# Weighted sum of two expert outputs: a ScalarE product in the first tile, and the last tile's stores as four pieces from SyncE's queue

## The chip, the cores and the metric

The kernel runs on one core of a Trainium2 chip. The core has five engines, of which this kernel computes with two: VectorE (DVE in the profile) and ScalarE (ACT). SyncE (SP) and ScalarE also issue transfers between the device memory (HBM) and the on-chip memory (SBUF); what each has issued stands in a queue of its own (in the profile q1 holds what SP issued, q10 what ScalarE issued), and 16 DMA engines work on both queues. The metric is the device time of one execution in microseconds (us); the time of a kernel is the median over its runs.

## The reference

For each of 16 x 1024 tokens there are two rows of 512 float32 numbers (the outputs of two experts) and two weights. The result is the weighted sum of the two rows.

```python
# expert_outputs (16, 1024, 2, 512), combine_weights (16, 1024, 2), all float32
weights = combine_weights[..., np.newaxis]
return np.sum(expert_outputs * weights, axis=2).astype(np.float32)
```

So 67.1 MB are read, 33.6 MB are written, and there are three floating-point operations for each number written.

## The kernel before, in words

The 16384 tokens are laid over 128 partitions: partition p holds tokens 128p to 128p + 127. All weights are loaded once into `wt` (line 43, issued from ScalarE's queue, 128 KB).

The loop of line 45 goes over 16 tiles of J = 8 tokens per partition. A tile is loaded by one transfer of 4 MB into `et` (line 48, issued from SP). Each of its 8 tokens then takes two instructions on 128x512 elements:

- the product of the first expert's row and its weight, written to `ot`: on VectorE in tiles 0 to 14 (line 57), on ScalarE in the last tile (line 55);
- the product of the second row and its weight, added to it, in one VectorE instruction (line 58).

Tiles 0 to 14 leave by one store of 2 MB each (line 66, issued from ScalarE's queue). The last tile leaves in three stores of 4, 2 and 2 tokens (1 MB, 512 KB, 512 KB), from ScalarE's queue too. In the text, "load 15" is the load of the last tile, "store 14" the last 2 MB store, and tiles and loads count from 0.

Both pools hold four buffers (lines 39 and 40). So load g waits until VectorE is through with tile g - 4, and the products of tile g may only overwrite an `ot` that store g - 4 has read out. The framework puts the waits in and settles the order on each engine, which need not be that of the program text: in the last tile the trace shows six ScalarE products (tokens 0 to 5), then the stores of 4 and of 2 tokens, then the products of tokens 6 and 7, then the last store. An engine works through its own instructions in that order, so that a store that waits for VectorE holds the products behind it on ScalarE.

ScalarE needs a table in place before its first activation. The load of that table is an instruction that the compiler adds ahead of the first `activation` (it stands under line 55 too).

Of the kernel before, what the change touches and what calls it, by code (L numbers as in the profile page):

```python
# [1 line left out]

# [4 lines left out]


@with_exitstack
def kernel(  # L10
    ctx: ExitStack,
    tc: tile.TileContext,
    expert_outputs: bass.AP,
    combine_weights: bass.AP,
    out: bass.AP,
):


    nc = tc.nc
    b, s, k, h = expert_outputs.shape  # L20
    assert k == 2
    n = b * s
    P = nc.NUM_PARTITIONS
    per = n // P
    assert per * P == n
    eo = expert_outputs.rearrange("b s k h -> (b s) (k h)").rearrange("(p t) f -> p t f", p=P)
    cw = combine_weights.rearrange("b s k -> (b s) k").rearrange("(p t) k -> p (t k)", p=P)
    o = out.rearrange("b s h -> (b s) h").rearrange("(p t) f -> p t f", p=P)

    dt = mybir.dt.float32  # L30
    mult = mybir.AluOpType.mult
    add = mybir.AluOpType.add

    J = 8
    copy = mybir.ActivationFunctionType.Copy
    last = per // J - 1

    wpool = ctx.enter_context(tc.tile_pool(name="w", bufs=1))
    ipool = ctx.enter_context(tc.tile_pool(name="in", bufs=4))
    opool = ctx.enter_context(tc.tile_pool(name="out", bufs=4))  # L40

    wt = wpool.tile([P, per * k], dt)
    nc.scalar.dma_start(out=wt, in_=cw)

    for g in range(per // J):
        et = ipool.tile([P, J, k * h], dt)
        ot = opool.tile([P, J, h], dt)
        nc.sync.dma_start(out=et, in_=eo[:, g * J : (g + 1) * J, :])  # L48
        c0 = 0
        for c in (4, 2, 2) if g == last else (J,):  # L50
            for i in range(c0, c0 + c):
                t = g * J + i
                w0, w1 = wt[:, 2 * t : 2 * t + 1], wt[:, 2 * t + 1 : 2 * t + 2]
                if g == last:
                    nc.scalar.activation(out=ot[:, i, :], in_=et[:, i, 0:h], func=copy, scale=w0)  # L55
                else:
                    nc.vector.tensor_scalar_mul(out=ot[:, i, :], in0=et[:, i, 0:h], scalar1=w0)  # L57
                nc.vector.scalar_tensor_tensor(  # L58
                    out=ot[:, i, :],
                    in0=et[:, i, h : 2 * h],  # L60
                    scalar=w1,
                    in1=ot[:, i, :],
                    op0=mult,
                    op1=add,
                )
            nc.scalar.dma_start(  # L66
                out=o[:, g * J + c0 : g * J + c0 + c, :], in_=ot[:, c0 : c0 + c, :]
            )
            c0 += c


# [1 line left out]
_INS = ['expert_outputs', 'combine_weights']  # L73
_OUTS = [((16, 1024, 512), 'float32')]


# [23 lines left out]
```

## Time and profile before

Three runs took 241.24, 241.34 and 241.75 us; the median is 241.34 us. The profiled execution took 241.88 us, with a span of 240.1 us on the core, so 1.8 us lie around the span.

| What | us or rate |
|---|---|
| span of the profiled execution | 240.1 |
| VectorE busy | 133.8 (56%) |
| ScalarE busy | 6.4 (3%) |
| mean transfer rate over the span | 420 GB/s |
| weights in SBUF, VectorE's first instruction | 13.92 |
| first store issued | 22.51 |
| load 15 landed | 227.7 |
| table load, last tile | 227.81 to 229.09 |
| last store issued | 236.54 |

How to read it: times count from the start of the span. A row of groups names the line, the engine, the operation, what it writes and reads, the count, the busy time, the mean of one in ns, and the idle time of the engine ahead of it with what ended it. "Waits" are put down to what came last. The share of the DMA engines is the mean over the 16 of the time that their packets took; it can stand a little over 1, since packets overlap. A transfer's "time to landing" runs from its issue until the last of its 16 parts has reported. The row "queue 14, instruction" counts packets that carry instructions to the engines.

### The profile page before, as it was taken

The numbers are of one execution on the slowest core, as the hardware profiler recorded it, in microseconds if no ns is written. First come the engines' busy times: TensorE is split into PE (matmuls) and PEld (weight loads), VectorE is DVE, ScalarE is ACT, GpSimd is POOL, SyncE is SP. The second block draws the span as 40 slices with busy tenths as digits, with TensorE's granted clock in tenths as the row PEclk, the third lists the DMA queues.
The fourth block names the chain that finished last, engine by engine and source line by source line (L and its number), as shares of the span: only waits on it lengthen the run. The fifth ranks groups of instructions, "written<-read, shape, count | busy, mean of one in ns | idle before, by whom it ended". The sixth has DMA issues, their size and how long they took to land.

```text
span 240.1 us, 377 instructions
## 1 busy us (share of the span) xinstructions
DVE 133.8 (56%) x248; ACT 6.4 (3%) x9; POOL 0.2 (0%) x4
## 2 busy tenths in 40 slices
DVE  0068937729185490945819276391853919549062
ACT  0000000000000000000000000000000000000072
POOL 0000000000000000000000000000000000000000
DMA  7999999999999999999999999999999999999967
GB/s 267 439 434 431 355 434 456 414 431 437 437 423 445 439 409 426 456 415 453 420 437 431 415 448 423 431 450 437 435 423 434 420 429 442 418 450 437 412 296 304
DMA packets 5042, 100.81 MB, mean 420 GB/s; under 512 B 560, under 2 KB 688, under 8 KB 944
## 3 DMA queue, kind: packets, MB, share of 16 engines
q1 hardware_dynamic: 2304, 67.11, 65.4%
q10 hardware_dynamic: 2736, 33.69, 32.9%
q14 instruction: 2, 0.02, 0.0%
HBM read 67.24 MB, written 33.55 MB: 420 GB/s over the span
## 4 chain that ended last, share of the span: by engine, by line
DMA 56%; DVE 26%; another core or an unknown queue 13%; issue 1%; ACT 1%; SPq 0%; ACTq 0%; DVEq 0%
DMA et<-in_expert_outputs_dram 56%; DVE ot L58 16%; DVE ot L57 10%; ACT ot L55 1%; ACT L55 1%; SPq L48 0%; ACTq L66 0%; DVEq L95 0%; DVEq L57 0%; ACTq L55 0%
## 5 line engine op out<-in xcount | busy, mean ns | idle before, releaser
L57 DVE TENSOR_SCALAR ot<-et,wt 128x512 f32<-128x512 f32 x120 | 52.7, 482 | 93.4 <-DMA et<-in_expert_outputs_dram 79.5
L58 DVE SCALAR_TENSOR_TENSOR ot<-et,wt,ot 128x512 f32<-128x512 f32 x128 | 90.0, 746 | 9.3 <-ACT ot L55 9.3
L55 ACT ACT_TABLE_LOAD x1 | 1.3, 1283 | 227.8 <-DMA et<-in_expert_outputs_dram 227.8
L55 ACT ACTIVATE ot<-et,wt 128x512 f32<-128x512 f32 x8 | 5.1, 709 | 1.5 <-DVE ot L58 1.5
L84 POOL MEMSET const-bfloat16-1.0<- 128x1 bf16 x1 | 0.1, 101 | 0.0
L84 POOL MEMSET const-uint8-127<- 128x1 uint8 x1 | 0.1, 101 | 0.0
L84 POOL MEMSET const-float32-0.0<- 128x1 f32 x1 | 0.1, 98 | 0.2 <-issue 0.2
L84 POOL MEMSET const-float32-1.0<- 128x1 f32 x1 | 0.1, 98 | 0.0
## 6 DMA issues: line engine op xcount, KB each, us to landing
et<-in_expert_outputs_dram SPq DMA_DIRECT2D x16, 4096.0 KB, 49.6
out_dram<-ot ACTq DMA_DIRECT2D x15, 2048.0 KB, 24.9
out_dram<-ot ACTq DMA_DIRECT2D x1, 1024.0 KB, 3.9
out_dram<-ot ACTq DMA_DIRECT2D x2, 512.0 KB, 3.2
wt<-in_combine_weights_dram ACTq DMA_DIRECT2D x1, 128.0 KB, 13.2
```

The source lines that it names most:

```text
L55: nc.scalar.activation(out=ot[:, i, :], in_=et[:, i, 0:h], func=copy, scale=w0)
L57: nc.vector.tensor_scalar_mul(out=ot[:, i, :], in0=et[:, i, 0:h], scalar1=w0)
L58: nc.vector.scalar_tensor_tensor(out=ot[:, i, :], in0=et[:, i, h : 2 * h], scalar=w1, in1=ot[:, i, :], op0=mult, op1=add,)
L84: nc = _bacc.Bacc("TRN2", target_bir_lowering=False, num_devices=1)
```

## The change

Two things change. First, the product of token 0 of tile 0 goes from VectorE to ScalarE, by the same `activation` that the last tile uses; the compiler's table load then stands ahead of this one. Second, the last tile's stores are of 2, 2, 2 and 2 tokens (512 KB each) instead of 4, 2 and 2, and they are issued from SP's queue instead of ScalarE's. The sums, the other 119 VectorE products, the loads and the stores of tiles 0 to 14 stay as they were.

```diff
-        for c in (4, 2, 2) if g == last else (J,):
+        for c in (2, 2, 2, 2) if g == last else (J,):
             for i in range(c0, c0 + c):
                 t = g * J + i
                 w0, w1 = wt[:, 2 * t : 2 * t + 1], wt[:, 2 * t + 1 : 2 * t + 2]
-                if g == last:
+                if t == 0 or g == last:
                     nc.scalar.activation(out=ot[:, i, :], in_=et[:, i, 0:h], func=copy, scale=w0)
                 else:
                     nc.vector.tensor_scalar_mul(out=ot[:, i, :], in0=et[:, i, 0:h], scalar1=w0)
...
-            nc.scalar.dma_start(
+            (nc.sync if g == last else nc.scalar).dma_start(
                 out=o[:, g * J + c0 : g * J + c0 + c, :], in_=ot[:, c0 : c0 + c, :]
             )
```

More of the change, by code (lines that the diff above doesn't have):

```diff
@@ L32 @@
     add = mybir.AluOpType.add
+    copy = mybir.ActivationFunctionType.Copy
     J = 8
-    copy = mybir.ActivationFunctionType.Copy
     last = per // J - 1
```

## The prediction, made before the changed kernel ran

> **What bounds the kernel now.** I read the page first: the busy times, the slices of the span and the queues.
>
> ```profile
> DVE 133.8 (56%) x248; ACT 6.4 (3%) x9; POOL 0.2 (0%) x4
> ...
> DMA  7999999999999999999999999999999999999967
> GB/s 267 439 434 431 355 434 456 414 431 437 437 423 445 439 409 426 456 415 453 420 437 431 415 448 423 431 450 437 435 423 434 420 429 442 418 450 437 412 296 304
> ...
> q1 hardware_dynamic: 2304, 67.11, 65.4%
> q10 hardware_dynamic: 2736, 33.69, 32.9%
> q14 instruction: 2, 0.02, 0.0%
> ```
>
> VectorE idles 44% of the span; the DMA engines are busy in every slice but the first and the last two (0.98 of 16 engines' span). So the kernel moves bytes, and time can be won only where DMA engines stand idle: at the start, and in the last 12 us, where the rate falls to 296 and 304 GB/s. The change works on the last. The end of the chain of waits (start, length, what) shows how that stretch runs:
>
> ```profile
> 227.72 0.02 issue
> 227.74 0.04 ACTq L55
> 227.78 0.03 issue
> 227.81 1.28 ACT L55
> 229.09 0.01 issue
> 229.10 0.73 ACT ot L55
> 229.83 0.02 issue
> 229.85 4.08 DVE ot L58 x6
> 233.93 0.02 issue
> 233.95 0.34 ACTq L66
> 234.29 0.05 issue
> 234.34 0.73 ACT ot L55
> 235.07 0.03 issue
> 235.09 0.75 DVE ot L58
> ```
>
> Load 15 lands at 227.72. The table load (1.28 us) comes before the first product, and later ScalarE's products of tokens 6 and 7 stand behind the second store's issue, so that VectorE waits 1.17 us after its sixth sum. Read alone, this chain says that both waits can be taken out whole. I therefore asked what the DMA engines do meanwhile; the view by stretches of time gives the busy time of the engines, the clock, the DMA share and GB/s:
>
> ```profile
> 228.00:231.00 3.00, 1.15 (x2) 2.99 (x5) 0.00 (x0) 1.00 0.98 421
> 231.00:232.00 1.00, 1.00 (x3) 1.00 (x3) 0.00 (x0) 1.00 0.54 229
> 232.00:233.00 1.00, 1.00 (x2) 0.88 (x2) 0.00 (x0) 1.00 0.08 33
> 233.00:234.00 1.00, 0.92 (x2) 0.00 (x0) 0.00 (x0) 1.00 0.63 262
> 234.00:236.00 2.00, 0.91 (x2) 1.33 (x2) 0.00 (x0) 1.00 0.97 395
> ```
>
> After the load is in, older stores still fill the engines until 231 or so; a hole of about 1.5 us follows, and then the last tile's stores run at full rate to the end. But 0.08 in 232 to 233 is not zero: it is one of 16 engines, still at work. The trace's packet records, which no view prints, say so: 15 engines finish their part of store 14 between 231.4 and 232.6, the sixteenth at 233.36. The first packets of the last tile's stores start at 233.47 to 233.62 on all 16. For that engine there is hardly a hole, and a store has landed only when its slowest sixteenth has.
>
> Where its lag comes from: the two instruction packets (8 KB each) start at 47.4 and 173.7. Up to the load that landed at 168.7 the last of the 16 parts reports within 0.06 us of the one before it; from the load landed at 184.1 on it is 0.90 us behind. A fetch thus delays one engine by 0.85 to 0.9 us. The change takes away one of VectorE's instructions of 248, so I expect both fetches to stay.
>
> **The change part by part.** *The table load leaves the last tile:* ScalarE's first product there starts at 227.82 instead of 229.10, 1.28 us sooner.
>
> One rule can be weighed here. The Trainium skill, "ScalarE: Activation LUTs", section "What ACT_TABLE_LOAD costs", gives 1283 ns for the load, as this trace has it, and adds a drain of about 1380 ns, 2.66 us in total. By the page the first product would come 2.66 us sooner; the trace has the product 0.01 us after the load, with no drain between, so 1.28 is used. With 2.66 the limit by computing would move 1.38 us further, and the sum, which the slowest DMA engine sets, would stay.
>
> *The stores leave ScalarE's queue:* its eight products run through, and VectorE's 1.17 us wait goes. Six sums took 4.08 us, a step of (4.08 - 0.75)/5 = 0.666; eight take 5.41. First product 227.82 to 228.55, first sum at 228.57, eighth done at 233.98 instead of 236.51. Pieces are ready after sums 2, 4, 6 and 8: 229.98, 231.31, 232.65, 233.98.
>
> *Four issues on SP, three fewer on ScalarE:* SP's 328 ns row for a load's issue is near ScalarE's 338 for a store's. SP's last load issue ends at 177.7, and nothing but the final waits stands behind, so these issues hold nobody. The weights' issue and stores 0 to 14 stay in ScalarE's queue; POOL's four constants are over at 0.4. From issue to first packet took 0.84 us (232.63 to 233.47) and 0.87 (236.54 to 237.41). The old stores lie in q10, the new in q1; both take turns on the same 16 engines, so crossing over doesn't change what an engine has left to do.
>
> *The 1 MB store becomes two of 512 KB:* per engine 8 packets of 0.313 (2.50 us) become 16 of 0.160 (2.56): 0.06 us more, and one completion more (0.01). That this store's fixed time to landing adds to the end is bounded by zero (the pieces queue behind each other, as the second 512 KB did, landing 3.9 us after issue but 1.3 after the 1 MB) and by 2.6 - 1.3 = 1.3 us, the last store's 2.6 less its data time. I take zero, by the nearest row: the last tile's own queue.
>
> A rule speaks against this part. The Trainium skill, "DMA: Bandwidth & Descriptors", section "Rules for kernel authors", wants at least 1 MiB per DMA for full bandwidth, and its fit has 2.0 us fixed for each; paid once more and not overlapped, the time would come out near 243.0. The trace's two 512 KB stores ran at 385 to 395 GB/s behind a 1 MB one, so the sum has none of it.
>
> *Both limits of the tail.* By computing: last issue 234.01, first packet 234.88, eight packets 1.28: data out at 236.16 instead of 238.84, 2.68 us sooner. By the slowest engine: store 14 done at 233.36, then 4 x 8 packets of 0.160 and completions: 233.36 + 5.12 + 0.04 = 238.52, 0.32 us sooner. The later one decides: 0.3 us. Its other ends are 2.7 (no lagging engine) and 0, if some 0.3 us of gaps between pieces return.
>
> *The first tile's new wait.* The weights are there at 13.92; then ScalarE takes 1.28 and 0.73, so the first sum starts at 15.95. VectorE saves one product (0.44 in its pairs of 0.88) of the 8.56 us that tile 0 took (13.92 to 22.48). If it waits idle, it ends at 15.95 + 8.12 = 24.07, 1.6 late; if one product is put ahead of the wait, 1.15 late. Behind it stand load 4's issue (SP) and store 0's (ScalarE), both 1.15 to 1.6 us later than 22.51. Cover: loads 1 to 3 fill the queue until 52; tile 1 starts up to 0.6 later than 23.46, and VectorE then waits for load 2 until 37.74, so the delay is gone by tile 2. Work left undone by stores is done by loads, so cost zero. Without that cover it is up to 1.6 us; and a gain isn't excluded either: where the first store comes in, the rate falls to 311 and 336 GB/s (24 to 28 us), (430 - 324)/430 x 4 = 1.0 us lost against the usual 430. This may be lost again, in part, or doubled: -1.0 to +1.0. I take zero, since the same first store enters the same full queue.
>
> Sum: -0.3 on the profiled execution (span 240.1 to 239.8, time 241.88 to 241.6). That execution stands 0.54 above the median of 241.34, so the forecast for the median is 241.0.
>
> **The rivals.** *B, the lag is smaller.* If the engine that fetches isn't the one that is last anyway, the next slowest (232.58) decides: 0.78 us more, 240.3. For it: two fetches that land at another moment. Against: both fetches exist in any version.
>
> *C, computing decides.* If all engines are through by 232, the whole 2.7 us come: 238.7. Against it stands the record at 233.36.
>
> *D, slower: the first store's entry.* At 24 to 28 us, the later store 0 meets another phase of the loads; the dip grows, or the fetching engine falls in with those 0.8 us behind at landing (two or three engines are, from 37 on). A dip twice as long costs 1.0, net +0.7: 242.0. It decides from a loss of 0.8 us upward. For it: such a dip stands in the trace only there, and its cause isn't shown. Against: the engines have the same bytes.
>
> *E, nothing happens:* gaps eat the 0.3 us, 241.3.
>
> **How the numbers follow.** A measurement of this kernel can hardly tell less than 0.2% (0.48 us) from no change. Forecast A 0.45 (its own range 240.8 to 241.4, all within 0.2% but 0.03), B 0.24, C 0.08, D 0.17, E 0.06. Faster: B, C and 0.03 of A, 0.35. Same: 0.42 + 0.06 = 0.48. Slower: D, 0.17. For 8 in 10 the range leaves out C and most of D above 241.9, and takes in B with a 0.1 us margin: 240.2 to 241.9.
>
> **What would show it.** Table load at 14 us and none after 220; first sum near 15.9; load 4 and store 0 issued at 23.6 to 24.1; eight sums in 5.4 us without a gap; four issues on SP at 230.0 to 234.0; no slice under 0.3 DMA share before 237 but then a thinning tail, with one engine finishing alone near 238.5. Wrong, if the last pieces land with all engines together 1 us or more sooner (B, C), or if load 15 lands later than 227.9 (D).

## The result and the profile after

The changed kernel took 241.50 us (median of 6 runs, 241.32 to 241.57), the kernel before beside it 241.55 us (6 runs, 241.24 to 241.83). The ratio is 0.9997 with a 95% interval of 0.9984 to 1.0010: no difference. The profiled execution took 241.57 us with a span of 239.8, where the one of before had 241.88 and 240.1.

The page of the changed kernel, busy times, slices and queues:

```profile
DVE 133.3 (56%) x247; ACT 7.0 (3%) x10; POOL 0.2 (0%) x4
...
GB/s 268 440 435 410 394 415 448 450 432 402 424 446 421 456 432 437 418 456 405 421 437 443 421 456 435 437 418 424 430 424 459 424 437 437 437 407 440 413 420 209
...
q1 hardware_dynamic: 2880, 69.21, 67.6%
q10 hardware_dynamic: 2304, 31.59, 30.8%
q14 instruction: 2, 0.02, 0.0%
```

2.1 MB have gone over from q10 to q1. The last slice but one is full now (420 for 296 GB/s) and the last is emptier (209 for 304): the same bytes, moved earlier. The two instruction packets are still there. The end of its chain of waits:

```profile
227.81 0.02 issue
227.84 0.02 ACTq L57
227.85 0.04 issue
227.90 0.73 ACT ot L57
228.63 0.03 issue
228.65 4.73 DVE ot L60 x7
```

Both waits are gone: no table load between the landing of load 15 (227.81) and the first product, and no gap in the sums. By the list of instructions in order of time the eight sums take 5.39 us and the stores are issued from 230.09 on, the last at 234.07, against 236.54 before. Computing ends 2.5 us sooner; the span ends 0.3 us sooner. The view by stretches (busy time of the stretch, VectorE, ScalarE, POOL, clock, DMA share, GB/s) shows what lies between:

```profile
232.00:233.00 1.00, 1.00 (x3) 0.90 (x2) 0.00 (x0) 1.00 1.05 430
236.00:237.00 1.00, 0.00 (x0) 0.00 (x0) 0.00 (x0) 1.00 0.73 299
237.00:238.00 1.00, 0.00 (x0) 0.00 (x0) 0.00 (x0) 1.00 0.06 25
238.00:238.50 0.50, 0.00 (x0) 0.00 (x0) 0.00 (x0) 1.00 0.06 25
238.50:239.80 1.30, 0.00 (x0) 0.00 (x0) 0.00 (x0) 1.00 0.00 0
```

The hole at 232 is filled. A new one stands at the end: from 237 to 238.5 the share is 0.06, one sixteenth, at 25 GB/s. One DMA engine works alone. By the trace's landing records, which no view prints, 15 parts of the last store report between 236.72 and 237.47, the sixteenth at 238.81; and the sixteenth part of store 14 lands at 233.88, 1.37 us behind the fifteenth. So an engine was late before the last tile began, and no order of the last tile's work takes anything from it. The records don't number the engines: that it is the same one each time is read from the lag (the last part's distance to the fifteenth), which stays from landing to landing.

In the first tile (in order of time; start, length):

```profile
13.77 1.28 ACT L57 ACT_TABLE_LOAD   x1 [13.77 <-DMA et<-in_expert_outputs_dram]
13.89 0.88 DVE L59 TENSOR_SCALAR ot<-et,wt 128x512 f32<-128x512 f32 x2 [13.89 <-DMA wt<-in_combine_weights_dram]
14.69 1.41 DVE L60 SCALAR_TENSOR_TENSOR ot<-et,wt,ot 128x512 f32<-128x512 f32 x2
15.06 0.72 ACT L57 ACTIVATE ot<-et,wt 128x512 f32<-128x512 f32 x1
...
22.09 0.37 ACTq L69 DMA_DIRECT2D out_dram<-ot  x1
```

VectorE doesn't wait for ScalarE: products and sums of two other tokens come first, and store 0 is issued at 22.09, where it was 22.51.

### The profile page after: what moved, and what is told of

The parts are those of the page before. It is cut to its first block, busy times and chain, and to the rows that moved or that the text cites. A ratio compares the mean times of both kernels' runs of the same rounds, so it can differ in the third digit from the quotient of the medians.

```text
span 239.8 us, 381 instructions
## 1 busy us (share of the span) xinstructions
DVE 133.3 (56%) x247; ACT 7.0 (3%) x10; POOL 0.2 (0%) x4
## 4 chain that ended last, share of the span: by engine, by line
DMA 56%; DVE 26%; another core or an unknown queue 13%; issue 1%; SPq 0%; ACT 0%; DVEq 0%; ACTq 0%
DMA et<-in_expert_outputs_dram 56%; DVE ot L60 16%; DVE ot L59 10%; SPq L48 0%; ACT ot L57 0%; DVEq L98 0%; ACTq L69 0%; DVEq L59 0%; ACTq L57 0%
## 5 line engine op out<-in xcount | busy, mean ns | idle before, releaser
L59 DVE TENSOR_SCALAR ot<-et,wt 128x512 f32<-128x512 f32 x119 | 52.3, 481 | 93.9 <-DMA et<-in_expert_outputs_dram 80.0
L57 ACT ACTIVATE ot<-et,wt 128x512 f32<-128x512 f32 x9 | 5.7, 709 | 212.1 <-DMA et<-in_expert_outputs_dram 212.1
```

## The experiments

The theory, T1: one DMA engine, made late by instruction packets, sets the end of both kernels. The rivals: T2, the packets or the lag have nothing to do with VectorE's instructions; T3, computing sets the end; T4, four stores cost a fixed price each that eats the gain.

**Each half of the change alone.** The table load:

```diff
-                if g == last:
+                if t == 0 or g == last:
```

> Only the first half of the change: the product of token 0 of tile 0 on ScalarE, the last tile's stores as before (4, 2, 2 tokens from ScalarE's queue). Theory T1 (one DMA engine, late by 1.4 us after two instruction packets, sets the end): the last tile's first store is issued 1.3 us sooner, at 231.35, but the late engine is through with store 14 at 233.4 as before and has 5.06 us of packets left, so the span is 239.6 to 240.0 and the ratio to before 0.997 to 1.001; in the tail one engine works alone for about 1 us. Rival T3 (no engine stands out, the chain of computing sets the end): 1.28 us sooner, ratio 0.995.

Ratio 0.9989 (0.9979 to 0.9998), 241.30 us, span 239.5. The stores, with the table load left in the last tile:

```diff
-                if t == 0 or g == last:
+                if g == last:
```

> Only the second half: four stores of 2 tokens from SP's queue, the table load still in the last tile. T1: first product at 229.10, pieces ready at 231.3 to 235.3, the late engine again decides, span 239.6 to 240.0, ratio 0.997 to 1.001. T3 (computing sets the end): the eighth sum comes 1.2 us sooner than before, ratio 0.995. A fixed price for each store (rival T4) would show as the last piece landing more than 1.5 us after the one before it, ratio over 1.002.

Ratio 0.9992 (0.9983 to 1.0000), 241.50 us, span 239.5. Each half alone reaches what both together reach, as T1 has it; T3's 0.995 lies outside both intervals, and neither half is more than 0.11% off the kernel before. The sixteenth part of store 14 lands at 233.71 and 233.63 in these two, as late as ever.

**Without the older stores.** Both kernels with stores 13 and 14 left out (4 MB of the result stay unwritten):

```diff
+            if g in (last - 2, last - 1):
+                continue
```

> The kernel before without stores 13 and 14 (4 MB of the output are left unwritten), so that no older store is in the queues when load 15 lands. T1: load 15 lands at 221 to 224; then the chain of computing runs as before, 12.4 us from its landing to the end, span 234 to 236.5, and the DMA engines stand idle until the first piece of the last tile.

> The changed kernel, again without stores 13 and 14 (4 MB of the output left unwritten). T1 (the gain of the change was hidden behind the older stores on the late engine): without them the whole 2.4 to 2.8 us come out, 9.6 to 10.0 us from load 15's landing to the end, about 1.0% less than the kernel of the same cut with the tail of before. Rival T4 (four stores on SP's queue cost what the earlier start gains): difference 0 to 0.5 us here too.

238.10 us (ratio 0.9861, 0.9844 to 0.9877) with the tail of before, 235.57 us (0.9756, 0.9740 to 0.9772) with the changed one: 2.53 us. From the landing of load 15 to the end it is 236.4 - 224.14 = 12.3 us and 233.8 - 224.06 = 9.7 us. By stretches, first the tail of before, then the changed one:

```profile
224.00:227.00 3.00, 0.72 (x2) 2.76 (x4) 0.00 (x0) 1.00 0.00 0
227.00:229.80 2.80, 2.80 (x6) 2.31 (x4) 0.00 (x0) 1.00 0.00 0
229.80:235.30 5.50, 1.96 (x3) 1.33 (x2) 0.00 (x0) 1.00 0.94 381
```

```profile
224.00:227.00 3.00, 2.10 (x4) 2.86 (x5) 0.00 (x0) 1.00 0.00 0
227.00:228.00 1.00, 1.00 (x2) 1.00 (x3) 0.00 (x0) 1.00 0.85 348
228.00:233.00 5.00, 2.29 (x4) 1.15 (x2) 0.00 (x0) 1.00 0.87 350
```

With nothing left in the queues the DMA engines wait, from that landing, 5.8 us for the first piece in one and 3.1 in the other. So the change does all that it says, 2.5 us of it, and what hides it in the whole kernel is the backlog of older stores, which the late engine works off last. T4 falls here, and again in the changed kernel itself, where the last parts of the four stores land at 235.10, 236.33, 237.57 and 238.81, 1.23 to 1.24 us apart: no more than their data time (eight packets of 0.159 us on each engine).

**One store instead of four.**

```diff
-        for c in (2, 2, 2, 2) if g == last else (J,):
+        for c in (J,):
```

> The changed kernel with one store of 8 tokens (2 MB, SP's queue) for the last tile. Limit by computing: the eighth sum ends near 234.0, first packet at 234.9, eight packets of 0.611 us per engine, out at 239.8, span near 241.1, ratio to before 1.002 to 1.006. If a fixed price for each store counted (T4), three prices saved would make it faster than the changed kernel.

Ratio 1.0048 (1.0031 to 1.0066), 242.69 us, span 240.9. By stretches:

```profile
232.00:233.00 1.00, 1.00 (x2) 0.69 (x2) 0.00 (x0) 1.00 0.08 33
233.00:234.00 1.00, 0.82 (x2) 0.00 (x0) 0.00 (x0) 1.00 0.00 0
234.00:235.00 1.00, 0.00 (x0) 0.00 (x0) 0.00 (x0) 1.00 0.62 262
235.00:239.80 4.80, 0.00 (x0) 0.00 (x0) 0.00 (x0) 1.00 0.90 382
```

Now even the late engine is done (233.26) before the store's first packet (234.70), and computing sets the end. The data is out at 239.78, 1.3 us past the late engine's limit in the changed kernel (238.47): here pieces help until the late engine decides, and no further.

**What makes the engine late.** In the changed kernel's landing records, the last part of a load or store comes at most 0.10 us behind the fifteenth until 41 us, 0.45 to 0.59 from the load that landed at 52.5 on, and 1.28 to 1.49 from the one at 184.2 on. The instruction packets start at 47.49 and 173.82. The second packet shows in all eight profiles that have two, near 47 and 173 us (both kernels, each half, the one store, the two without the older stores, the second profile of before): the lag of the loads, of the stores or of both grows by 0.5 to 1.0 us behind it. The first shows clearly in about half of them, and not in the profile of before, where the last part of a load is 0.17 us behind at 37.7 and 0.06 at 52.3. For more packets, products and sums of tiles 1 to 10 were done in halves:

```diff
+                elif 1 <= g <= 10:
+                    for a in (0, h // 2):
+                        nc.vector.tensor_scalar_mul(
+                            out=ot[:, i, a : a + h // 2], in0=et[:, i, a : a + h // 2], scalar1=w0
+                        )
...
```

> The changed kernel with 160 VectorE instructions more and the same results: in tiles 1 to 10 each product and each sum is done in two halves of 256 columns. VectorE stays under the 14.5 us that a tile has. T1 (the instruction packets follow VectorE's count and delay one engine): at least a third packet, one engine 0.6 to 0.9 us later again, span 240.3 to 240.7, ratio to before 1.001 to 1.004, where the changed kernel has 0.9997. If the packet falls on another engine than the late one: no change in time. Rival T2 (packets at set times): two packets, at 47 and 174, ratio as the changed kernel.

```profile
q1 hardware_dynamic: 2880, 69.21, 67.5%
q10 hardware_dynamic: 2304, 31.59, 30.8%
q14 instruction: 3, 0.02, 0.0%
```

Three packets, at 36.5, 96.0 and 154.5; ratio 1.0028 (1.0019 to 1.0037), 242.07 us, span 240.3, 0.5 above the changed kernel's. When they start, VectorE has begun 50, 181 and 313 of the instructions that the trace records: 131 and 132 apart. In the changed kernel it has begun 50 and 196, 146 apart. So they follow VectorE's progress through its instructions, if not one fixed count of recorded ones, and T2's set times fall. The lag itself didn't grow: the last part of the last store is 1.26 us behind the fifteenth, for 1.34 in the changed kernel. But the last two parts land 0.5 to 0.6 us later than there, the fourteenth only 0.1: two engines are later now.

For none of them, tiles 0 to 14 took two wide VectorE instructions each, with the changed tail and with that of before (beside the lines shown, the last tile's products are set behind the issue of store 14 on ScalarE):

```diff
+        if g < last:
+            ev = et.rearrange("p j (k h) -> p (j k) h", k=k)
+            wb = wt[:, 2 * J * g : 2 * J * (g + 1)].unsqueeze(2).to_broadcast([P, 2 * J, h])
+            nc.vector.tensor_tensor(out=ev, in0=ev, in1=wb, op=mult)
+            nc.vector.tensor_tensor(out=ot, in0=et[:, :, 0:h], in1=et[:, :, h : 2 * h], op=add)
+            st = nc.scalar.dma_start(out=o[:, g * J : (g + 1) * J, :], in_=ot)
+            continue
```

> The changed tail on a kernel with few VectorE instructions: tiles 0 to 14 take two wide instructions each (one product of the whole tile with the weights spread out, one sum of the halves) instead of 16, the table is loaded by a ScalarE activation on one column of the weights. VectorE has 38 such instructions instead of 247. T1, if the two instruction packets are VectorE's: none falls before the end (or only one), the 16 engines end store 14 within about 0.9 us of each other, the last data is out near 237.4, span 238.4 to 239.0, ratio 0.993 to 0.997. Rival T2 (the packets come at set times, or the engine is late for another reason): packets at 47 and 174 again, one engine alone at the end, ratio 0.999 to 1.001. Against both: the wide instructions take some 12.9 us of the 14.5 us that a tile has, and if they are slower than that VectorE becomes the bound and the ratio goes over 1.01.

> The tail of before on the same kernel with few VectorE instructions (no ScalarE activation ahead of the last tile). T1: with no late engine the chain of computing decides: table load, products 6 and 7 behind a store's issue, last store issued near 236.5 and out 2.3 us later; span 239.8 to 240.3, ratio 0.999 to 1.002, all engines idle together for over 1 us near 232 to 233.4. So the difference between this kernel and the one with the changed tail would be 1.1 to 1.7 us, where it was 0 with the late engine. T2: both as before and after, difference 0 to 0.3 us.

No instruction packet in either. With the changed tail 0.9971 (0.9958 to 0.9984), 241.00 us, span 239.2; with the tail of before 0.9957 (0.9944 to 0.9969), 240.69 us, span 238.8. That is a gain, as T1 has it, but the first lies just outside what was expected (span 238.4 to 239.0, ratio to 0.997): its parts of store 14 land from 231.69 to 233.88, six of them 0.55 us and more behind the other ten, and not within 0.9 us. So packets are not the only thing that sets engines apart. My expectation of the second failed outright. Stretches of the wide kernel with the tail of before show why:

```profile
229.00:231.00 2.00, 1.79 (x3) 0.76 (x2) 0.00 (x0) 1.00 1.07 459
231.00:232.00 1.00, 0.03 (x1) 0.79 (x2) 0.00 (x0) 1.00 0.81 344
232.00:233.00 1.00, 1.00 (x2) 0.55 (x1) 0.00 (x0) 1.00 1.01 426
233.00:234.00 1.00, 0.38 (x1) 0.00 (x0) 0.00 (x0) 1.00 0.95 401
```

There is no hole at 232. In this wide kernel load 15 lands at 221.4 instead of 227.7 (221.7 with the changed tail), the stores being further behind the loads; the last tile's first store is issued at 229.50, while the older stores still run, and the slow chain lies beside them. So the tail of the change is not needed there at all; and since the wide kernels differ in this too, their gain can't be put down to the missing packets alone.

Which half of the change makes the wide kernel 0.3 us slower, not faster, was tried with each half alone (the same kernel without the early activation, and with it but without the four stores on SP's queue):

> The kernel with wide VectorE instructions and, of the change, the four stores on SP's queue alone (no ScalarE activation ahead of the last tile). Open is why the wide kernel with the whole change (239.2 span, ratio 0.9971) came out behind the wide kernel with the tail of before (238.8, 0.9957), where five engines ended store 14 some 0.8 us behind the rest in the first. If the stores on SP's queue do it, this kernel stands at 0.997; if the early activation's effect on the start does it, at 0.9957; if it is chance from one execution to the next, in between, with single runs over 0.7 us apart.

> The wide kernel with, of the change, the early table load alone (an activation on one column of the weights ahead of the loop), the last tile's stores as before. If the early activation costs the 0.3 us: ratio 0.997, engines about 0.8 us apart at the end of store 14; if the stores on SP's queue cost it: 0.9957 or a little less.

241.01 us (0.9974, 0.9965 to 0.9984; span 239.3) with the stores alone, 240.62 us (0.9968, 0.9956 to 0.9981; span 238.8) with the table load alone. The two ratios don't tell them apart, but the single runs nearly do: 240.75 to 241.14 against 240.55 to 240.88. The early activation shows no cost; the 0.4 us come with the stores on SP's queue. How they come is open: in that kernel the last part of a load is 0.3 to 0.6 us behind the fifteenth from the load that lands at 137.4 on, some 90 us before the first of these stores is issued, and with no instruction packet in it; so it isn't the stores' own traffic.

Last, with all products on ScalarE:

```diff
-                if t == 0 or g == last:
+                if True:
```

> The changed kernel with all 128 products on ScalarE: VectorE has 128 instructions of its own instead of 247, ScalarE 119 more. T1: VectorE's second packet (at its instruction 196 or so) is never needed, the first falls near its instruction 50, later in time. If ScalarE's packets follow its own count and fall on another DMA engine, the late engine is 0.6 us behind the others instead of 1.4: span 239.0 to 239.5, ratio 0.995 to 0.999. If they fall on the same engine: ratio 0.999 to 1.001. ScalarE's stores of tiles 0 to 14 stand behind products there, which could delay them; ScalarE's 8 products of a tile take 5.0 us of 14.5.

Ratio 0.9967 (0.9958 to 0.9976), 240.72 us, span 239.4. Two instruction packets again, at 92.9 and 100.1, but the last part of the last store comes 0.61 us behind the fifteenth instead of 1.34. That fits one packet for VectorE and one for ScalarE, falling on two DMA engines, but it is inferred from the counts alone (VectorE has begun 58 and 65 recorded instructions at the two, ScalarE 62 and 69). The size of the lag doesn't prove it: the wide kernel with the four stores on SP's queue ends with a lag of 0.64 us and has no packet.

**The kernel before, once more.** Its 67 runs in this study fall into two groups, 36 from 241.04 to 241.44 and 31 from 241.65 to 242.09, with none between; the changed kernel's six, 241.32 to 241.57, lie between the groups' middles (241.27 and 241.85). The profile of before was of the upper group.

> The kernel before, unchanged, for a second profile. Its single runs fall into two groups, 241.0 to 241.4 and 241.6 to 242.1, and the profile shown was of the upper one (241.88). T1: if this one is of the lower group, the late engine ends store 14 some 0.6 us sooner, near 232.7 instead of 233.36, the lag of the last sixteenth of store 14 is near 0.3 us instead of 0.8, and the span is near 239.5. If the lag is 0.8 at a span of 239.5, the two groups have another cause. If it falls in the upper group again, it says nothing on that.

This one was of the lower: 241.37 us, span 239.6. T1's expectation fell: the late engine ends store 14 at 233.37, as it did before (233.36). What differs is the landing of load 15, as the chain of waits of this second profile shows:

```profile
227.15 0.02 issue
...
227.24 1.28 ACT L55
...
233.38 0.34 ACTq L66
233.72 0.05 issue
233.77 0.73 ACT ot L55
```

Load 15 lands at 227.15 instead of 227.72, and everything after it stands 0.57 us sooner. The last store's data is out at 238.32 instead of 238.84. Here both limits meet: the last part of the last store is only 0.06 us behind the fifteenth, where those of the two stores ahead of it were 0.27 and 0.22 behind. So in the upper profile computing sets the end, 0.3 to 0.5 us past the late engine's limit (238.3 to 238.5), and T1 doesn't hold for it; in the lower one the two tie. The changed kernel's profile stands on the late engine's limit (238.47). The two profiles of before also differ in where the lag lies: from 184 us on the last part of the loads is 0.85 to 0.90 us behind in the upper, 0.31 to 0.36 in the lower; that of the stores landing between 187 and 218 us is at most 0.06 behind in the upper, 1.07 to 1.25 in the lower. Both end store 14 at the same time, and load 15 comes sooner where the stores have the lag. What decides between the two is open, and this is one profile of each group, no more.

## Why the prediction was right, and where it wasn't

- *The bound.* Right. The step "for that engine there is hardly a hole" carried the forecast, and the runs show it: each half alone and both together end within 0.11% of before, while without older stores the change is worth 2.53 us (2.68 by the sum's limit of computing). That the upper profile of before itself ends by computing is in the prediction's two limits.
- *The sum.* Data out at 238.52 by the sum, 238.47 measured; span 239.8 and 239.8; 241.6 for the profiled execution, 241.57 measured. Computing: last issue at 234.01 by the sum, 234.07 measured.
- *The median.* 241.0 was forecast, 241.5 measured, 0.2% off. It is inside the range because the range is wide; it lies outside forecast A's own 240.8 to 241.4 and looks like E, "nothing happens", though not by E's gaps: the four stores follow each other without any. The step that failed is "that execution stands 0.54 above the median of 241.34, so the forecast for the median is 241.0". It took 0.54 as an offset that both kernels share. It is the distance between two groups of the kernel before, and the change wins 0.3 us only against the upper: against the lower, 241.37 in its second profile, it wins nothing.
- *The first tile.* Wrong: "both 1.15 to 1.6 us later than 22.51" was 0.42 us sooner. The sum let VectorE wait, or put one product ahead; the scheduled order has products and sums of two tokens ahead, 2.1 us of work, beside ScalarE's 2.0, and tile 0 is shorter by the product that it gave away. Its price in the sum, zero, holds all the same: the kernel with this half alone took 0.9989 of before.
- *The entry of the first store.* 393 GB/s in both stretches from 24 to 28 us, for 311 and 336: by the same working 0.6 us of DMA time less lost. It wasn't in the sum and didn't come out in the end; the second profile of before has 344 and 352 there. The mean over 16 engines says little about the one that is late.
- *The packets of instructions.* Right that both stay. "A fetch thus delays one engine by 0.85 to 0.9 us" was read from the second packet alone; the first left nothing of the kind in that profile, and 0.47 us in the changed kernel, where the second left 1.0. (The prediction's "within 0.06 us" up to 168.7 also passes over a load that was 0.17 behind, at 37.74.) Rival B's 0.78 us did not come, and C has no trace in the runs: store 14's last part lands at 233.6 to 233.9 in all the kernels with VectorE's two packets and store 14 in place. D has none either: load 15 landed at 227.81, before D's 227.9.
- *The rule on large transfers.* With the four stores of 512 KB the DMA engines moved 406 to 430 GB/s from 232 to 236 us, and with one of 2 MB the kernel was slower, by 0.5% against before. The rule, which the prediction set aside by the trace, does not help at this kernel's end; no run here splits the transfers of its middle. The 2.0 us of the fit did not show; the page gives that fit for transfers that GpSimd issues, and these came from SP.

The Trainium skill, "Runtime: NRT & Kernel Launch", section "Instruction fetch mechanics", calls the cost of going on to the next block of instructions mostly hidden. VectorE, idle 44% of the time here, has room for it. The DMA engine that carries the packets had none: three instead of two went with 0.3% more, and none, in kernels that differ in more than that, with 0.3 to 0.4% less.

The wide kernel with the early table load, 240.62 us, and the one with the tail of before, 240.69, are faster than the kernel before, by 0.3 to 0.4% against its runs beside them, and so than the changed one, which equals it.

## What to carry to other kernels

Where the DMA engines bound a kernel, a gap in their mean share isn't time that can be won until one knows that every engine has it: ask when the last sixteenth of the store before it lands, and add the bytes still to come. To see whether a change of the tail does its work at all, take the backlog away that covers it. And before a difference of tenths of a per cent is reasoned from one profile, look at how the single runs lie: here the profile was of one group and the median of the other.

## What the runs showed that I had not expected

- VectorE's instruction count costs DMA time: one packet of 8 KB for each 131 to 146 recorded instructions. The second one left the last part of a load or store 0.5 to 1.0 us later, though the packet itself takes 0.31; why it is more than that is open. 160 instructions more cost 0.5 us of span, though VectorE still stood idle for 36% of it.
- The kernel before has two groups of times 0.5 us apart, and the changed kernel's six runs lie between their middles, so that the median hardly moves.
- In the wide kernels VectorE is busy 84% of the span instead of 56%, and they are the faster ones.
